# Both experts of a pair in one 16 KB home: 2 MB weight loads in a one-core decoder block

## The chip, the core and the metric

The kernel runs on one core of a Trainium2 chip. Its time is the device time of one execution in microseconds (us), the median of three runs. "MB" is 1,048,576 bytes and "KB" 1,024 where loads are counted; the profile's own GB/s and MB are decimal.

## What is computed

One decoder block on 256 tokens of width 1024, all in float32. Cut to what matters:

```python
h = rmsnorm(x, norm_mix_g) * (1 + scale_m) + shift_m           # scale, shift, gate from c @ w_ada
x = x + gate_m * mixer(h, positions, w_in, ...)                # mLSTM and retention, merged by gates
h = rmsnorm(x, norm_ffn_g) * (1 + scale_f) + shift_f
x = x + gate_f * moe(h, ...)
return rmsnorm(x, norm_final_g)

def moe(xm, ...):                                              # 32 experts, the best 4 for each token
    top_val, top_idx = lax.top_k(xt @ w_router + b_router, 4)
    top_w = softmax(top_val)
    # for each expert e, over the tokens that chose it
    gu = xb @ w_gate_up[e] + b_gate_up[e]                      # 1024 x 2048
    y = clamped_swiglu(gu) @ w_down[e] + b_down[e]             # 1024 x 1024
    # summed over each token's experts, weighted by top_w
```

The experts' weights are 32 x 12 MB = 384 MB and are read once.

## The kernel before, in words

The kernel has two stages. The first, up to line 1032, is the mixer with its modulation weights, the output projection and the routing. The second, from line 1035, runs over the 32 experts in 16 pairs. An expert has 64 slots for tokens; the pair's 128 slots fill PE's output rows, expert q in rows 64q to 64q+63.

**Homes.** All large weights go through one set of regions of 8 KB per partition, 1 MB each. There are 22 of them, named W0a, W0b, ... U6b, 11 names with two halves each. A table `ready` keeps a number for each half: the turn at which it was last filled or set free. `oldest` (line 138) returns the halves with the smallest numbers, whatever their names; `place` (line 129) puts a weight there, and `wslot` (line 144) places a weight of 2 MB in two halves and loads each with one DMA on SP's queue. The mixer's weights (w_in, the branches, wout, and the modulation weights wada) are loaded by `wslot`; in the mixer some halves also hold activations (U1 to U6, Z), and `free` enters them into the table when those are done. A load into a half waits until the last reader of what was there is done.

**The expert stage.** Each pair has four gate-and-up blocks (`gu`, n = 0 to 3) of 512 columns and two down blocks (`dn`, n = 0 and 1). A block is 4 MB: two experts, each with two halves of 1 MB (half h holds rows 512h to 512h+511 of the weight, as 128 partitions x 4 row groups x 512 columns). `both` (line 1156) takes four homes and issues four loads on SP, in the order (h=0,q=0), (h=0,q=1), (h=1,q=0), (h=1,q=1). In memory each of these is its own block of 128 rows of 8 KB. A name such as gu1531b in the profile is pair 15, block 3, expert 1, second half.

PE goes through k = 0 to 7 and, within each k, through q = 0, 1 (line 1204 for gate-and-up, 1245 for down): k = 0 to 3 read the first halves, k = 4 to 7 the second. Between the products PE turns the activations of the block before (`fill`), and in the second down block it gathers the next pair's tokens (`step`, line 1073). SP's order of loads in this stage and PE's order are as written in the code; the order of DVE and ACT in most of the mixer is not.

**The last pair.** Its first down block is loaded in eight pieces of 512 KB (runs of 4 KB, lines 1235 to 1239), its second one in sixteen pieces of 256 KB (runs of 2 KB) from a separate array `tail`, laid out so that its columns come in three cuts, `TAIL` (0 to 256, 256 to 384, 384 to 512). The output is normalised cut by cut (`finish`, line 1123).

**Overfull experts.** From line 1290 there is a branch for experts with more than 64 tokens. It repeats the work in a loop; in the profile it is skipped.

Of the kernel before, what the change touches and what calls it, by code (L numbers as in the profile page):

```python
# [10 lines left out]
F32 = mybir.dt.float32  # L11
# [9 lines left out]
D = 1024  # L21
T = 256
# [48 lines left out]
class Weight:  # L71


    def __init__(self, tiles, dim=1):
        self.tiles, self.dim = tiles, dim
# [11 lines left out]
class Pieces:  # L87


    def __init__(self, tiles, cuts):  # L90
        self.tiles, self.cuts = tiles, cuts

    def __getitem__(self, at):
        _, k, cs = at
        n, off = divmod(8 * cs.start, 2048)
        width = cs.stop - cs.start
        assert (cs.start, cs.stop) in self.cuts and off + 8 * width <= 2048
        off += k * width
        return self.tiles[n].rearrange("p a b -> p (a b)")[:, off:off + width]
# [3 lines left out]
def block(ctx, tc, I, out, dbg=None):  # L103
# [5 lines left out]
    big = ctx.enter_context(tc.tile_pool(name="big", bufs=1))  # L109
# [8 lines left out]

    ready = {f"W{i}{h}": 0 for i in range(4) for h in "ab"}
    clock = [0]  # L120

    def region(tag, shape, name, dt=F32, pool_=big):
        return pool_.tile(shape, dt, name=name, tag=tag)
# [5 lines left out]
    def place(tags, name, dim=1, pool_=big, cuts=((0, 512),)):  # L129
# [5 lines left out]
        tiles = [region(tag, half, name + h, pool_=pool_) for tag, h in zip(tags, "ab")]  # L135
        return Weight(tiles, dim) if len(cuts) == 1 else Pieces(tiles, cuts)
# [898 lines left out]
    w1, w2 = blocks_of("w1"), blocks_of("w2")  # L1035
# [120 lines left out]
    def both(src, name):  # L1156

        tags = oldest(4)
        w = [place(tags[q::2], f"{name}{q}") for q in range(2)]
        for h in range(2):  # L1160
            for q in range(2):
                ready[tags[2 * h + q]] = clock[0] + 0.25 * h
                sp.dma_start(flat(w[q].tiles[h]), src(q)(h))
        return w

    def gu(pair, n):
        return both(lambda q: w1(2 * pair + q, n), f"gu{pair}{n}")

    def dn(pair, n):
        return both(lambda q: w2(2 * pair + q, n), f"dn{pair}{n}")  # L1170
# [13 lines left out]
    for pair in range(NP):  # L1184
# [41 lines left out]
        for n in range(2):  # L1226
            if not last:
                w = dn(pair, n)
                cuts = ((0, 512),)
            else:  # L1230

                cuts = TAIL if n else ((0, 512),)
                w = [place(oldest(), f"dn{pair}{n}{q}", cuts=cuts) for q in range(2)]
                size = 512 if n else 1024
                for i in range(0, 4096, size):
                    for q in range(2):
                        h, c = divmod(i, 2048)
                        src = I["tail"][q, h] if n else w2(2 * pair + q, n)(h)
                        sp.dma_start(flat(w[q].tiles[h])[:, c:c + size], src[:, c:c + size])
            for c0, c1 in cuts:  # L1240
# [4 lines left out]
                for k in range(8):  # L1245
                    for q in range(2):
                        pe.matmul(p[q * CAP:(q + 1) * CAP, :c1 - c0], aT[:, k, q * CAP:(q + 1) * CAP], w[q][:, k, c0:c1],  # L1247
                                  start=False, stop=k == 7, skip_group_check=True)
# [28 lines left out]
        if pair == NP - 2:  # L1277
            tags = oldest()
            x2 = region(tags[0], [128, 2, D], "x2")
            gno = region(tags[1], [128, 2, D], "gno")  # L1280
            gn = gno[:, 0]
            for tag in tags:
                del ready[tag]
            waiting.append(lambda: row_of(cols[:, GFIN:GFIN + 8], gn, "gn", tr))
# [6 lines left out]
    with tc.If(more > 0):  # L1291
# [5 lines left out]
        with tc.For_i(0, E, 1) as e:  # L1297
# [3 lines left out]
            dve.tensor_copy(pcur, posm[:, :, ds(e, 1)].rearrange("p t o -> p (t o)"))  # L1301
            dve.tensor_copy(wcur, wm[:, :, ds(e, 1)].rearrange("p t o -> p (t o)"))
            dve.tensor_copy(sel, id3[:, ds(e, 1)].to_broadcast([96, CAP]))
            n_e = nc.values_load(nb[0:1, ds(e, 1)], min_val=0, max_val=T // CAP - 1)
            with tc.For_i(0, n_e, 1) as b:
# [21 lines left out]
                for n in range(4):  # L1327
                    w = wslot(lambda h: I["w1"][ds(e, 1), n, h].rearrange("o p c -> (o p) c"), f"gux{n}")
# [7 lines left out]
                    for q in range(2):  # L1336
                        pe.transpose(p[:, q * CAP:(q + 1) * CAP], a[:CAP, q * 128:(q + 1) * 128], ident[:CAP, :CAP])
                    act.activation(aT[:, 2 * n:2 * n + 2].rearrange("p k s -> p (k s)"), p[:, :2 * CAP], AF.Copy)
                for n in range(2):
                    ns = slice(n * 512, (n + 1) * 512)  # L1340
                    w = wslot(lambda h: I["w2"][ds(e, 1), n, h].rearrange("o p c -> (o p) c"), f"dnx{n}")
# [6 lines left out]
                    for t in range(2):  # L1348
                        pe.matmul(yacc[t][n], cwT[:, t * 128:(t + 1) * 128], yp, start=False, stop=True,
                                  skip_group_check=True)  # L1350

# [30 lines left out]
def arranged(inputs):  # L1382
# [17 lines left out]
    arrays["w1"] = halves(apart(I["w_gate_up"][0]))  # L1400
    w2 = I["w_down"][0]
    arrays["w2"] = halves(w2)
    last = w2[E - 2:, :, 512:].reshape(2, 8, 128, 512).swapaxes(1, 2)
    tail = [last[:, :, :, c0:c1].reshape(2, 128, -1) for c0, c1 in TAIL]
    tail = np.concatenate(tail, axis=2).reshape(2, 128, 2, 2048).swapaxes(1, 2)
# [20 lines left out]
```

## Time and profile before

| | us |
|---|---|
| three runs | 1266.93, 1266.97, 1268.28 |
| median | 1266.97 |
| the profiled execution | 1265.93 |
| its span, first to last instruction | 1263.8 |
| mean granted clock of TensorE | 0.993 of full speed |

The profile is of one execution. PE is TensorE's matmul, PEld its weight loads, DVE is VectorE, ACT ScalarE, SP the engine that issues the loads; "SPq" is its queue. A row of a timeline gives the start (us from the span's start), the duration, the engine and the line of the code, and the tile that is written, with what it reads. The duration of a DMA row is that of the issue on SP and not of the transfer. The chain of waits is followed back from the last instruction; a piece that is called DMA in it lasts from the issue of a load to its landing.

### The profile page before, as it was taken

What the parts mean: (1) busy time and instruction counts of PE and PEld (TensorE: products, weight loads), DVE (VectorE), ACT (ScalarE), POOL (GpSimd) and SP (SyncE); (2) the same over time, 40 slices, a digit from 0 to 9 for tenths busy, and PEclk for the clock granted to TensorE, in tenths of its full rate; (3) what the DMA queues carried; (4) which work ended last, traced back from release to release, by engine and by line L of the source; (5) the groups of instructions that cost most, each with busy time, mean ns of one, the idle gap of its engine ahead of it and who ended that gap; (6) DMA issues with size and microseconds to landing.
All of it is one profiled execution on the core that took longest, in us unless ns stands there. A gap on an engine that the chain in (4) does not pass through costs nothing.

```text
span 1263.8 us, 14948 instructions
## 1 busy us (share of the span) xinstructions
PE 1205.4 (95%) x5872; PEld 606.2 (48%) x5873; DVE 491.2 (39%) x1167; ACT 289.5 (23%) x559; POOL 3.9 (0%) x14
## 2 busy tenths in 40 slices
PE   8999999999899999999999999998999999999995
PEld 6878888878534334344343334343434333333333
DVE  5599889878422222222222222121212131222124
ACT  4585555565211101111010101010101011010111
POOL 0000000000000000000000000000000000000000
PEclk9999999999899999999999999999999999999998
DMA  9955788858799999999999999999999999999995
GB/s 363 362 185 212 291 291 330 360 203 332 274 422 422 421 420 422 421 420 420 421 422 421 422 421 421 421 422 421 421 421 421 421 421 421 422 421 420 421 410 183
DMA packets 72607, 479.13 MB, mean 379 GB/s; under 512 B 8786, under 2 KB 9746, under 8 KB 17492
## 3 DMA queue, kind: packets, MB, share of 16 engines
q1 hardware_dynamic: 71668, 477.54, 92.9%
q8 instruction: 47, 0.77, 0.2%
q10 hardware_dynamic: 864, 0.59, 0.2%
q14 instruction: 28, 0.23, 0.1%
HBM read 476.46 MB, written 1.05 MB: 378 GB/s over the span
## 4 chain that ended last, share of the span: by engine, by line
DMA 49%; PE 46%; DVE 3%; ACT 1%; issue 0%; SPq 0%; ACTq 0%; DVEq 0%
PE gup L1206 12%; PE dnp L1247 6%; PE xgp L1078 2%; DMA gu1331b<-in_w 2%; DMA gu511a<-in_w 2%; DMA gu911a<-in_w 2%; DMA dn511a<-in_w 2%; DMA dn911a<-in_w 2%; DMA gu1411b<-in_w 2%; DMA gu611a<-in_w 2%; DMA gu1011a<-in_w 2%; DMA dn811a<-in_w 2%; DMA dn1211a<-in_w 2%; DMA gu1231a<-in_w 2%; DMA gu1531b<-in_w 2%; DMA gu1131a<-in_w 2%
## 5 line engine op out<-in xcount | busy, mean ns | idle before, releaser
L1114 DVE TENSOR_SCALAR g<-gup 128x256 f32<-128x256 f32 x64 | 27.2, 425 | 354.6 <-PE gup L1206 354.6
L1195 ACT ACTIVATE aT<-aTp 128x256 f32<-128x256 f32 x64 | 24.6, 384 | 292.9 <-PE aTp L1194 292.9
L1078 PEld LDWEIGHTS xgp<-oh,x 128*128 128x128 f32 x512 | 63.5, 195 | 51.4 <-issue 26.0
L1115 ACT ACTIVATE sg<-g 128x256 f32<-128x256 f32 x64 | 26.7, 417 | 256.2 <-DVE g L1114 253.0
L1084 DVE TENSOR_SCALAR xg<-xgp,fsc,fsh 128x128 f32<-128x128 f32 x64 | 26.2, 409 | 149.1 <-ACT xg L1086 149.1
L1078 PE MATMUL xgp<-oh,x 128*128 128x128 f32 x512 | 75.5, 292 | 1.0 <-DVE oh L1070 1.0
L1254 DVE SCALAR_TENSOR_TENSOR yp<-dnp,wsl,gf 128x512 f32<-128x512 f32 (+2 forms) x34 | 24.5, 719 | 113.0 <-PE dnp L1247 110.9
L1086 ACT ACTIVATE xg<-xgp,fsh,fsc 128x128 f32<-128x128 f32 x64 | 29.0, 454 | 156.6 <-PE xgp L1078 156.6
L1264 ACT ACTIVATE yph<-yp 128x512 fp32r<-128x512 f32 x31 | 19.5, 629 | 94.7 <-DVE yp L1254 94.7
L1194 PEld LDWEIGHTS aTp<-ca,a 128*128 128x128 f32 x128 | 13.8, 141 | 39.5 <-issue 39.5
L1118 DVE TENSOR_TENSOR a<-a,sg 128x256 f32<-128x256 f32 x64 | 27.2, 425 | 8.2 <-ACT sg L1115 1.0
L1270 PE MATMUL ya<-yph,ohT 128*128 128x512 f32 x62 | 27.8, 449 | 1.5 <-ACT yph L1264 1.5
L1117 DVE SCALAR_TENSOR_TENSOR a<-a,g 128x256 f32<-128x256 f32 x64 | 27.2, 425 | 2.1
L1194 PE MATMUL aTp<-ca,a 128*128 128x128 f32 x128 | 27.4, 296 | 0.0
L1116 DVE TENSOR_SCALAR a<-gup 128x256 f32<-128x256 f32 x64 | 26.6, 415 | 0.0
L1265 DVE TENSOR_TENSOR ypl<-yp,yph 128x512 fp32r<-128x512 f32 x31 | 21.4, 689 | 11.9 <-ACT yph L1264 11.9
L1104 DVE TENSOR_SCALAR ohT<-cwp 128x256 fp32r<-128x256 f32 x16 | 6.8, 425 | 48.7 <-PE cwp L1103 48.7
L202 PE MATMUL gup<-bex,id 96*64 96x512 bf16 x128 | 25.1, 387 | 0.0
L1270 PEld LDWEIGHTS ya<-yph,ohT 128*128 128x128 f32 x62 | 11.6, 187 | 28.2 <-issue 24.3
L1270 PE MATMUL ya<-ypl,ohT 128*128 128x512 f32 x62 | 24.6, 397 | 0.2 <-DVE ypl L1265 0.2
L202 PEld LDWEIGHTS <-id 96*64 96x64 bf16 x196 | 12.3, 109 | 23.9 <-issue 20.5
L1070 DVE TENSOR_SCALAR oh<-ca,posm,rc 128x64 f32<-128x64 f32 x64 | 17.0, 309 | 6.3 <-PE xgp L1078 6.3
(1280 smaller groups left out, 3223.8 us busy)
## 6 DMA issues: line engine op xcount, KB each, us to landing
x<-in_x SPq DMA_DIRECT2D x2, 512.0 KB
wada2a<-in_ada SPq DMA_DIRECT2D x2, 512.0 KB, 7.6
wada0a<-in_ada SPq DMA_DIRECT2D x2, 512.0 KB, 8.9
wfirst0a<-in_win SPq DMA_DIRECT2D x2, 512.0 KB, 10.6
wfirst1a<-in_win SPq DMA_DIRECT2D x2, 512.0 KB, 10.1
wada2b<-in_ada SPq DMA_DIRECT2D x2, 512.0 KB
wfirst2a<-in_win SPq DMA_DIRECT2D x2, 512.0 KB, 10.2
wada0b<-in_ada SPq DMA_DIRECT2D x2, 512.0 KB, 10.2
```

The source lines that it names most:

```text
L202: pe.matmul(p[rows, :c1 - c0], id3[:, e:e + 1].to_broadcast([96, CAP]), bex[:, n, c0:c1], start=True, stop=False, skip_group_check=True)
L1078: pe.matmul(p[:, q * 128:(q + 1) * 128], x[:, t, k * 128:(k + 1) * 128], oh[:, t].rearrange("p q s -> p (q s)"), start=t == 0, stop=t == 1)
L1086: act.activation(xg[:, k], pq, AF.Identity, bias=fsh[:, k:k + 1], scale=fsc[:, k:k + 1])
L1114: dve.tensor_scalar(g[:r], v[:, 0], LIMIT, None, op0=OP.min)
L1115: act.activation(sg[:r], g[:r], AF.Sigmoid, scale=ALPHA)
L1116: dve.tensor_scalar(a[:r], v[:, 1], LIMIT, -LIMIT, op0=OP.min, op1=OP.max)
L1117: dve.scalar_tensor_tensor(a[:r], a[:r], 1.0, g[:r], op0=OP.add, op1=OP.mult)
L1118: dve.tensor_mul(a[:r], a[:r], sg[:r])
L1194: pe.transpose(p[:, q * 128:(q + 1) * 128], a[:, q * 128:(q + 1) * 128], ident)
L1206: pe.matmul(p[q * CAP:(q + 1) * CAP], xg[:, k, q * CAP:(q + 1) * CAP], w[q][:, k], start=False, stop=k == 7, skip_group_check=True)
L1247: pe.matmul(p[q * CAP:(q + 1) * CAP, :c1 - c0], aT[:, k, q * CAP:(q + 1) * CAP], w[q][:, k, c0:c1], start=False, stop=k == 7, skip_group_c ...
L1270: pe.matmul(yacc[t][n], ohT[:, t * 128:(t + 1) * 128], part, start=pair == i == 0, stop=i == 1 and pair >= NP - 2, skip_group_check=True)
```

## The change

A home is now a whole name: 11 homes of 16 KB per partition. In the mixer `oldest` returns the two halves of the name whose later half has the smallest number. After the routing the set of regions is closed, and a new one, `pairs`, is opened with 11 tiles of 16 KB; `home` takes them in a fixed rotation, first the one that came free first. The weights of a pair are rearranged in memory (outside the timed kernel): half h of both experts lies in one block of 128 rows of 16 KB, expert 0's 8 KB and then expert 1's. A block (`block_of`) is loaded by two DMAs of 2 MB instead of four of 1 MB. `Pairs` finds expert q's rows in the tile. The last pair's first down block is loaded like every other, in two loads of 2 MB; its second one in eight pieces of 512 KB with runs of 4 KB, each of which holds both experts' part. `x2` and `gno` take one home of 16 KB where they took two of 8 KB. The branch for overfull experts loads an expert's half as two pieces and goes through pairs, with the two experts of a pair written out one after the other.

The diff, cut to its core:

```diff
+class Pairs:
+    def __init__(self, tiles):
+        self.tiles = tiles
     def __getitem__(self, at):
-        _, k, cs = at
...
+        q, k, cs = at
+        off = q * 2048 + k % 4 * 512
+        return self.tiles[k // 4][:, off + cs.start:off + cs.stop]
+
+class Pieces(Pairs):
+    def __getitem__(self, at):
+        q, k, cs = at
         width = cs.stop - cs.start
...
+        tile, off = divmod(8 * cs.start, 2048)
+        step, row = divmod(k, 512 // width)
+        off = (off if tile else 0) * 2 + step * 1024 + q * 512 + row * width
+        return self.tiles[tile][:, off:off + width]
...
-    def oldest(n=2):
-        return sorted(ready, key=lambda t: (ready[t], t))[:n]
+    def whole():
+        return {n: max(ready[n + "a"], ready[n + "b"]) for n in NAMES if n + "a" in ready and n + "b" in ready}
+
+    def oldest():
+        free = whole()
+        name = min(free, key=lambda n: (free[n], n))
+        return [name + "a", name + "b"]
...
-    w1, w2 = blocks_of("w1"), blocks_of("w2")
+    bctx.close()
+    pairs = ctx.enter_context(tc.tile_pool(name="pairs", bufs=1, reuse_waits="tile"))
+    queue = sorted(NAMES, key=lambda n: (whole()[n], n))
+
+    def pair_tile(tag, name):
+        return pairs.tile([128, 4096 + MORE.get(tag, 0)], F32, name=name, tag=tag)[:, :4096]
+
+    for name in NAMES:
+        pair_tile(name, f"pair{name}")
+
+    def home(name):
+        tag = queue.pop(0)
+        queue.append(tag)
+        return pair_tile(tag, name)
...
-    def both(src, name):
-        tags = oldest(4)
-        w = [place(tags[q::2], f"{name}{q}") for q in range(2)]
+    def block_of(src, name):
+        tiles = [home(f"{name}{h}") for h in "ab"]
         for h in range(2):
-            for q in range(2):
-                ready[tags[2 * h + q]] = clock[0] + 0.25 * h
-                sp.dma_start(flat(w[q].tiles[h]), src(q)(h))
-        return w
+            sp.dma_start(tiles[h], src[h])
+        return Pairs(tiles)
...
-                    pe.matmul(p[q * CAP:(q + 1) * CAP], xg[:, k, q * CAP:(q + 1) * CAP], w[q][:, k],
+                    pe.matmul(p[q * CAP:(q + 1) * CAP], xg[:, k, q * CAP:(q + 1) * CAP], w[q, k, slice(0, 512)],
...
-            if not last:
-                w = dn(pair, n)
-                cuts = ((0, 512),)
+            cuts = ((0, 512),)
+            if last and n:
+                cuts = TAIL
+                w = Pieces([home(f"tail{h}") for h in "ab"])
+                for h in range(2):
+                    for c in range(0, 4096, 1024):
+                        sp.dma_start(w.tiles[h][:, c:c + 1024], I["tail"][h, :, c:c + 1024])
             else:
-                cuts = TAIL if n else ((0, 512),)
-                w = [place(oldest(), f"dn{pair}{n}{q}", cuts=cuts) for q in range(2)]
-                size = 512 if n else 1024
-                for i in range(0, 4096, size):
-                    for q in range(2):
-                        h, c = divmod(i, 2048)
-                        src = I["tail"][q, h] if n else w2(2 * pair + q, n)(h)
-                        sp.dma_start(flat(w[q].tiles[h])[:, c:c + size], src[:, c:c + size])
+                w = dn(pair, n)
...
+    paired = lambda w: np.ascontiguousarray(w.reshape(E // 2, 2, -1, 2, 128, 2048).transpose(0, 2, 3, 4, 1, 5)).reshape(
+        E // 2, -1, 2, 128, 4096)
```

## Rows read from the trace of the kernel before

**Rows 1.** The page: busy PE, rate by slice, packets, one queue.

```profile
PE 1205.4 (95%) x5872; PEld 606.2 (48%) x5873; DVE 491.2 (39%) x1167; ACT 289.5 (23%) x559; POOL 3.9 (0%) x14
...
GB/s 363 362 185 212 291 291 330 360 203 332 274 422 422 421 420 422 421 420 420 421 422 421 422 421 421 421 422 421 421 421 421 421 421 421 422 421 420 421 410 183
DMA packets 72607, 479.13 MB, mean 379 GB/s; under 512 B 8786, under 2 KB 9746, under 8 KB 17492
...
q8 instruction: 47, 0.77, 0.2%
```

**Rows 2.** Windows: us, busy of PE, PEld, DVE, ACT, POOL; clock, DMA share, GB/s.

```profile
330.00:340.00 10.00, 10.00 (x54) 5.55 (x55) 3.01 (x11) 1.83 (x4) 0.00 (x0) 0.91 0.57 223
...
341.00:601.00 260.00, 258.79 (x1256) 97.60 (x1254) 67.97 (x178) 33.38 (x73) 0.00 (x0) 1.00 1.01 420
601.00:1226.00 625.00, 594.26 (x2668) 229.14 (x2664) 139.98 (x352) 64.94 (x147) 0.00 (x0) 1.00 1.01 421
...
1224.70:1236.30 11.60, 10.32 (x48) 3.13 (x45) 1.61 (x4) 1.18 (x3) 0.00 (x0) 1.00 0.95 365
```

**Rows 3.** The chain: start us, us, what; pairs 3 and 4, the passing-over, the last.

```profile
494.02 4.29 PE gup L1206 x20
...
546.33 4.29 PE gup L1206 x20
...
581.06 20.57 DMA gu511a<-in_w
...
1206.94 19.85 DMA gu1531b<-in_w
```

**Rows 4.** Issues on SP, every eighth load of the expert stage: start us, us.

```profile
1167.18 0.33 SPq L1163 DMA_DIRECT2D dn1411b<-in_w  x1
...
1187.06 0.33 SPq L1163 DMA_DIRECT2D gu1511b<-in_w  x1
...
1206.94 0.33 SPq L1163 DMA_DIRECT2D gu1531b<-in_w  x1
```

**Rows 5.** Issues on SP: the 22nd load of the expert stage and the 23rd.

```profile
323.74 0.76 SPq L1163 DMA_DIRECT2D dn011a<-in_w  x1
337.08 0.33 SPq L1163 DMA_DIRECT2D dn010b<-in_w  x1
```

**Rows 6.** Waits of PE from 60 to 330 us, the longest: total, times, longest.

```profile
PE pos L1026 <- DVE mask L1024: 1.8, 1, 1.8
```

**Rows 7.** Issues on SP at the start: first and last of ten 512 KB loads.

```profile
23.04 0.33 SPq L244 DMA_DIRECT2D wfirst0b<-in_win  x1
...
34.56 0.33 SPq L244 DMA_DIRECT2D wfirst2b<-in_win  x1
```

**Rows 8.** Issues on SP at the end; eight issues lie from each to the next.

```profile
1226.81 0.33 SPq L1239 DMA_DIRECT2D dn1501b<-in_w  x1
...
1236.84 0.33 SPq L1239 DMA_DIRECT2D dn1511a<-in_tail  x1
...
1242.01 0.33 SPq L1239 DMA_DIRECT2D dn1511b<-in_tail  x1
```

**Rows 9.** The chain, PE in the last pair's down blocks: start us, us, what.

```profile
1231.22 3.44 PE dnp L1247 x16
...
1235.02 3.79 PE dnp L1247 x16
...
1250.75 1.78 PE dnp L1247 x32
```

**Rows 10.** The tile gm: ns min/median/max, first and last start us, forms.

```profile
L310 DVE SCALAR_TENSOR_TENSOR gm<-wada4a,csil,gm x4: 745/748/752, 165.9 to 169.3; 128x512 f32<-128x512 f32 x4
...
L197 PE MATMUL rs<-gm,ones x4: 590/592/592, 265.6 to 266.9; 128*128 128x512 f32 x4
```

**Rows 11.** The tile o1b, its last reader.

```profile
L352 DVE TENSOR_TENSOR partsb<-o1b,partsa x4: 684/687/694, 163.6 to 167.4; 128x512 fp32r<-128x512 f32 x4
```

**Rows 12.** Issue on SP of the first half of wada4.

```profile
158.12 0.33 SPq L148 DMA_DIRECT2D wada4a<-in_ada  x1
```

More of the change, by code (lines that the diff above doesn't have):

```diff
@@ L84, in __getitem__ @@
         return self.tiles[n][tuple(at)]
-class Pieces:
-    def __init__(self, tiles, cuts):
-        self.tiles, self.cuts = tiles, cuts
+class Pairs:
+    def __init__(self, tiles):
+        self.tiles = tiles
     def __getitem__(self, at):
-        _, k, cs = at
-        n, off = divmod(8 * cs.start, 2048)
-        width = cs.stop - cs.start
-        assert (cs.start, cs.stop) in self.cuts and off + 8 * width <= 2048
-        off += k * width
-        return self.tiles[n].rearrange("p a b -> p (a b)")[:, off:off + width]
+        q, k, cs = at
[4 more added lines that the diff above has]
+        q, k, cs = at
+        width = cs.stop - cs.start
+        assert (cs.start, cs.stop) in TAIL
+        tile, off = divmod(8 * cs.start, 2048)
+        step, row = divmod(k, 512 // width)
+        off = (off if tile else 0) * 2 + step * 1024 + q * 512 + row * width
+        return self.tiles[tile][:, off:off + width]
 @with_exitstack
@@ L115, in f32v, with region @@
         return ap.bitcast(F32)
+    NAMES = ("W0", "W1", "W2", "W3", "Z", "U3", "U5", "U6", "U1", "U2", "U4")
     ready = {f"W{i}{h}": 0 for i in range(4) for h in "ab"}
+    MORE = {"U1": 4, "U2": 8, "U4": 8}
+    for name in NAMES:
+        for h in "ba":
+            size = 2048 + (MORE.get(name, 0) if h == "a" else 0)
+            big.tile([128, size], F32, name=f"first{name}{h}", tag=name + h)
     clock = [0]
-    def region(tag, shape, name, dt=F32, pool_=big):
-        return pool_.tile(shape, dt, name=name, tag=tag)
+    def region(tag, shape, name, dt=F32):
+        return big.tile(shape, dt, name=name, tag=tag)
     def free(*tags):
@@ L127, in free, with place @@
             ready[tag] = clock[0] + 0.5
-    def place(tags, name, dim=1, pool_=big, cuts=((0, 512),)):
+    def place(tags, name, dim=1):
         clock[0] += 1
@@ L134, in place @@
         half = [128, 4, 512] if dim == 1 else [128, 8, 256]
-        tiles = [region(tag, half, name + h, pool_=pool_) for tag, h in zip(tags, "ab")]
-        return Weight(tiles, dim) if len(cuts) == 1 else Pieces(tiles, cuts)
-    def oldest(n=2):
-        return sorted(ready, key=lambda t: (ready[t], t))[:n]
+        return Weight([region(tag, half, name + h) for tag, h in zip(tags, "ab")], dim)
+    def whole():
[4 more added lines that the diff above has]
+        return [name + "a", name + "b"]
     def flat(t):
@@ L1277, in block @@
         if pair == NP - 2:
-            tags = oldest()
-            x2 = region(tags[0], [128, 2, D], "x2")
-            gno = region(tags[1], [128, 2, D], "gno")
+            x2, gno = home("end").rearrange("p (i t d) -> i p t d", i=2, t=2)
+            queue.pop()
             gn = gno[:, 0]
-            for tag in tags:
-                del ready[tag]
             waiting.append(lambda: row_of(cols[:, GFIN:GFIN + 8], gn, "gn", tr))
@@ L1296, in block, with beyond, load @@
                 pe.matmul(yacc[t][n], zero, gf[:, :512], start=True, stop=True)
-        with tc.For_i(0, E, 1) as e:
+        def beyond(pr, q):
+            of = lambda ap: ap.rearrange("p t (r q) -> p t r q", q=2)[:, :, ds(pr, 1), q].rearrange("p t o -> p (t o)")
+            one = lambda ap: ap.rearrange("p (r q) -> p r q", q=2)[:, ds(pr, 1), q]
+            def load(name, n):
+                w = home(f"{name}{n}{q}").rearrange("p (k c) -> p k c", k=8)
+                for h in range(2):
+                    src = I[{"gux": "w1", "dnx": "w2"}[name]][ds(pr, 1), n, h, :, q * 2048:(q + 1) * 2048]
+                    sp.dma_start(flat(w[:, 4 * h:4 * h + 4]), src.rearrange("o p c -> (o p) c"))
+                return w
             pcur = s.tile([128, 2], F32, name="pcur", tag="pcur", bufs=1)
@@ L1300, in block @@
             sel = s.tile([96, CAP], BF16, name="selx", tag="selx", bufs=1)
[L1301 to L1304, printed above, removed]
+            dve.tensor_copy(pcur, of(posm))
+            dve.tensor_copy(wcur, of(wm))
+            dve.tensor_copy(sel, one(id3).to_broadcast([96, CAP]))
+            n_e = nc.values_load(one(nb[:, :E]), min_val=0, max_val=T // CAP - 1)
             with tc.For_i(0, n_e, 1) as b:
@@ L1327, in block @@
                 for n in range(4):
-                    w = wslot(lambda h: I["w1"][ds(e, 1), n, h].rearrange("o p c -> (o p) c"), f"gux{n}")
+                    w = load("gux", n)
                     p = at(f"gupx{n}")
@@ L1335, in block @@
                     p = tr(f"aTpx{n}")
-                    for q in range(2):
-                        pe.transpose(p[:, q * CAP:(q + 1) * CAP], a[:CAP, q * 128:(q + 1) * 128], ident[:CAP, :CAP])
+                    for j in range(2):
+                        pe.transpose(p[:, j * CAP:(j + 1) * CAP], a[:CAP, j * 128:(j + 1) * 128], ident[:CAP, :CAP])
                     act.activation(aT[:, 2 * n:2 * n + 2].rearrange("p k s -> p (k s)"), p[:, :2 * CAP], AF.Copy)
@@ L1340, in block @@
                     ns = slice(n * 512, (n + 1) * 512)
-                    w = wslot(lambda h: I["w2"][ds(e, 1), n, h].rearrange("o p c -> (o p) c"), f"dnx{n}")
+                    w = load("dnx", n)
                     p = at(f"dnpx{n}")
@@ L1350, in block @@
                                   skip_group_check=True)
+        with tc.For_i(0, E // 2, 1) as pr:
+            for q in range(2):
+                beyond(pr, q)
         for c0, c1 in zip(FIN, FIN[1:] + (D,)):
@@ L1399, in arranged @@
     arrays["bgu"] = np.ascontiguousarray(apart(I["b_gate_up"][0]).reshape(E, 4, 512).swapaxes(0, 1).reshape(128, 512))
-    arrays["w1"] = halves(apart(I["w_gate_up"][0]))
+    paired = lambda w: np.ascontiguousarray(w.reshape(E // 2, 2, -1, 2, 128, 2048).transpose(0, 2, 3, 4, 1, 5)).reshape(
+        E // 2, -1, 2, 128, 4096)
+    arrays["w1"] = paired(halves(apart(I["w_gate_up"][0])))
     w2 = I["w_down"][0]
[L1402 to L1405, printed above, removed]
+    arrays["w2"] = paired(halves(w2))
+    last = w2[E - 2:, :, 512:].reshape(2, 8, 128, 512)
+    tail = []
+    for c0, c1 in TAIL:
+        rows = 512 // (c1 - c0)
+        piece = last[..., c0:c1].reshape(2, 8 // rows, rows, 128, c1 - c0)
+        tail.append(piece.transpose(3, 1, 0, 2, 4).reshape(128, -1))
+    tail = np.concatenate(tail, axis=1).reshape(128, 2, 4096).swapaxes(0, 1)
     arrays["tail"] = np.ascontiguousarray(tail)
```

12 lines of the change are left out of this document (7 added, 5 removed).

## The prediction

> **What bounds the kernel now.** I read the page first: from the twelfth of the forty slices to the next to last the transfer rate is flat at 420 GB/s and a little over [rows 1]. PE's 95% says less, because the two stages have different limits, so next come the windows by stage. From 341 to 1226 us the DMA share is 1.01 at 420 to 421 GB/s, with TensorE's granted clock at 1.00 [rows 2]: the expert stage moves 384 MB at one steady rate.
>
> Then the chain of waits. PE works through a pair of experts in 52.3 us (494.02 to 546.33) as long as the weights lie ready, and the chain runs over PE. At 581 us it passes to transfers, and near the end it is transfers alone [rows 3]. A load starts when the one eight before it has landed, and three such loads start 19.88 us apart [rows 4]: eight of 1 MB in 19.88 us is **2.485 us for 1 MB**, so a pair's 24 MB take 59.6 us against PE's 52.3. From there on time is bytes over rate, and PE has 7 us per pair to spare.
>
> When did this stream start? The first 22 loads fill the 22 homes up to 323.74 us; then the queue waits until PE lets the first home go, at 337.08 [rows 5], and the engines run dry meanwhile (share 0.57 from 330 to 340 [rows 2]). So the stream begins at PE's first release, and all that PE does before it (the mixer, the routing) comes on top. In the mixer PE's longest waits are for DVE, the longest 1.8 us, and none is for a load [rows 6].
>
> **The change, part by part.** *The loads.* Up to the last gate-and-up load there are 15 x 24 + 16 = 376 MB; 22 are in place at the first release, so 354 MB follow: 354 loads of 1 MB before, 177 of 2 MB after. The bytes are the same. What halves is the number of runs: 128 of 8 KB, 8 for each of 16 engines, against 128 of 16 KB. A run is one packet now: 72607 packets less 17492 under 8 KB leave 55115 of 8 KB [rows 1], and the 376 loads alone need 48128.
>
> What does a run cost beyond its bytes? No row has a 16 KB load; loads of shorter runs give a line. At the start the weights come as 512 KB loads, 128 runs of 4 KB: from 23.04 to 34.56 us nine follow each other, **1.280 us** each [rows 7]. From two of these to one of 1 MB the bytes stay and the time falls from 2.560 to 2.485, so a load costs 0.075 us besides 1.205 us for each 512 KB. A 2 MB load is then 0.075 + 4 x 1.205 = 4.895 us instead of 4.970, and **177 x 0.075 = 13.3 us** go.
>
> The other end comes from the last loads. Eight landings of 4 KB runs, read from the issues that they release, lie between 1226.81 and 1236.84: 1.254 us each. Eight of 2 KB runs (256 KB) lie between there and 1242.01: 0.646 us [rows 8]. From 4 to 8 KB that makes a fixed cost of 2 x 1.254 - 2.485 = 0.023 us (177 x 0.023 = 4.1 us saved), from 2 to 4 KB 2 x 0.646 - 1.254 = 0.038 us (6.7 us saved). I take 13.3, because the nine loads of the start stand in an even stream of their own kind, while the last ones change size under way and the DMA share falls to 0.95 there [rows 2]. The 4.1 goes into the range. Nothing below zero follows from these rows; what would give it is a rival.
>
> *Fewer issues.* 12 instead of 24 per pair on SP, 0.33 us each [rows 4]. SP waits for a landing between any two, so this is worth nothing. Eight loads under way are now 16 MB, and three homes (6 MB) are left to PE. Home N needs load N-11 consumed; that landed three loads (14.7 us) before the landing that lets N start, and PE takes 52.3/12 = 4.4 us for each of a pair's 12 half blocks, so the home is free in time. If PE were further behind, the queue would only get shorter than eight; it is empty only when PE is 22 MB behind, as before.
>
> *Landing in pieces of 2 MB.* PE's order takes step k of one expert, then of the other, so it already needed both experts' 1 MB for nearly all of a half block: zero while the stream runs. It is not zero at the **last pair**, whose first down block came in eight pieces of 512 KB and now comes in two of 2 MB. Before: gate-and-up landed at 1226.79 (19.85 us after its issue [rows 3]), PE's first down product began at 1231.22, the second half at 1235.02, the end came 3.79 us later, at 1238.81 [rows 9]. After: the halves land 4.90 and 9.79 us behind the last gate-and-up load, so the second half begins at +9.8 where it began at +8.2 (1235.02 - 1226.79): **1.6 us lost**. From there the chain to the output is PE's and DVE's and unchanged. The last 4 MB, now eight pieces of 4 KB runs, land by +9.8 + 8 x 1.28 = +20.0; PE, done with the first down block at +9.8 + 3.8 = +13.6, takes up the last quarter 11.9 us after that (1250.75 - 1238.81 [rows 9]), so their faster landing hides behind PE and gains nothing.
>
> *Homes in the mixer.* Whole names only: the first half of the modulation weight wada4 moves from a home freed by 158.12 us, when its load starts [rows 12], to the home of o1, whose second half is read until a split that begins at 167.4 [rows 11]. Wada4 is first used at 165.9 [rows 10]. Its first half would start when o1's first half is done, some microseconds after 158, so DVE could stand for up to about 4 us; but DVE's order there is not written by hand, and the row it makes (gm) is read by PE only at 265.6 [rows 10]. I take nothing and keep 0 to +4. Into the experts a 2 MB load starts at the later of the two releases; the last homes (Z) still fill at 323.74, land some 10 to 12 us later, and the first release at 337.08 is PE's. Zero. The branch for overfull experts is longer and not entered: zero.
>
> **Sum:** -13.3 + 1.6 = -11.7 us. The profiled execution took 1265.93 (span 1263.8 and 2.1 around it), which gives 1254.2; the median of the runs is 1.0 above it, so I forecast **1255.3 us**.
>
> **The rivals.**
> 1. *The fixed cost is small and the stream near its ceiling.* For it: 4 KB and 8 KB runs differ by 1% only in the last loads [rows 8]. Against it: the even stretch of the start [rows 7]. It gives -4.1 + 1.6, 1264.5, or with the 2 KB rows' 6.7 us 1261.9. The Trainium skill, page "DMA: Bandwidth & Descriptors", section "Why small descriptors are slow (HBM only)", puts about 3 cycles on each packet; with the 850 MHz of its section "Where 436 GB/s comes from" that is, as an estimate, 8 x 3.5 ns = 0.028 us a load, 5.0 us in all and 1263.6. By that rule, the start's 0.075 is too large and the last loads' 0.023 about right.
> 2. *Nothing is saved: a 16 KB run travels as two packets of 8 KB.* The rate stays and the lump is paid at the old rate (2 x 4.97 - 8.2 = 1.7 us): 1268.7, no measurable change. Against it: instruction fetch has 47 packets for 0.77 MB, 16 KB each [rows 1], so packets of that size do travel.
> 3. *Slower: the engines read 16 KB runs less well than 8 KB runs.* The place is every load after 337 us; it decides from a load of about 4.975 us on, since 177 x 0.005 and the 1.7 us make 2.5 us, 0.2%. If a long run were handled at the rate of the 4 KB loads of the start, 2 MB would take 4 x 1.280 = 5.12 us: +26.6 + 1.7, 1295. For it speaks only that no 16 KB load is in the rows; against it, that the time per byte falls with every doubling. The Trainium skill, the same page, section "Latency and other measured facts", has copies losing up to half their rate when the rows of a tile lie a large power of two apart, from 512 KB up, and advises contiguous tiles. By it, a contiguous 2 MB block with rows 16 KB apart is safe; no run here shows it.
> 4. *The mixer's tighter homes hold DVE up by 4 us*, with the loads as forecast: 1259.3, still faster.
>
> **How the numbers follow.** Forecast 62%, rival 1 15% (half of it faster, half the same), rival 2 10%, rival 3 8%, rival 4 5%. About 0.2% (2.5 us, 1264.4 to 1269.5) is what a measurement can tell from no change. Faster: 62 + 5 + 7 = 74%. Same: 8 + 10 = 18%. Slower: 8%. The range leaves out rivals 2 and 3 (18%). Its low end, 1252, is the forecast with 0.006 us more per load and 2 us from the mixer's order; its high end, 1267, is rival 1 with that order against it. The forecast's own range is 1252 to 1259.
>
> **What would show it.** Right: loads of 2 MB starting 8 x 4.895 = 39.2 us apart every eighth, GB/s near 428 where it was 421, packets down by some 26000 (24064 of them in the 376 loads), and a stream that still begins near 337. The second half of the last pair's first down block should begin near 9.8 us after the last gate-and-up landing. PE should still have idle time in each pair (58.7 against 52.3 us). Wrong: 2 MB loads at 4.97 us (rival 2), or between 4.90 and 4.95 (rival 1); more than 128 packets a load; a first release that has moved by more than 2 us; or waits of PE inside the mixer for a load.

## The result, and the profile after

| | before | after |
|---|---|---|
| median of four runs, us | 1267.14 | 1252.9 (1251.71 to 1255.89) |
| ratio, with its 95% interval | | 0.9889 (0.9871 to 0.9908) |
| the profiled execution, us | 1265.93 | 1252.83 |
| its span, us | 1263.8 | 1251.0 |

The changed kernel is 1.1% faster. The forecast was 1255.3 us; the median lies 2.4 us below it and inside the range of 1252 to 1267. The page's lines that answer to [rows 1]:

```profile
GB/s 362 366 184 212 292 275 359 353 185 333 318 425 428 427 428 426 429 426 428 427 428 427 427 427 429 428 426 427 428 429 427 427 427 427 430 427 427 427 422 117
DMA packets 43518, 479.12 MB, mean 383 GB/s; under 512 B 5554, under 2 KB 6514, under 8 KB 12212
```

The shape is the same, with a flat rate from the twelfth slice on, but it is flat at 427 to 428 where it was at 421. The packets fall by 29089. The forecast's "some 26000" are among them: 24064 in the 376 loads and 1792 in the last pair's down blocks. Nearly all of the rest, 3232 packets under 512 B (8786 before, 5554 after), was not forecast. They are 16 for each of the 202 DMAs that are gone (188 of the 376, 6 and 8 in the last pair's two down blocks): each load has one small packet on each of the 16 engines.

The windows of the expert stage, columns as in [rows 2]:

```profile
341.00:601.00 260.00, 258.82 (x1254) 97.78 (x1252) 66.55 (x175) 31.67 (x71) 0.00 (x0) 1.00 1.01 427
601.00:1213.00 612.00, 562.12 (x2668) 204.70 (x2666) 140.01 (x352) 65.31 (x148) 0.00 (x0) 1.00 1.01 427
```

The issues on SP (start us, duration us), answering to [rows 4, 5]:

```profile
319.11 0.42 SPq L1196 DMA_DIRECT2D dn01a<-in_w  x1
333.82 0.33 SPq L1196 DMA_DIRECT2D dn01b<-in_w  x1
...
1131.53 0.33 SPq L1196 DMA_DIRECT2D dn141b<-in_w  x1
...
1170.69 0.33 SPq L1196 DMA_DIRECT2D gu153b<-in_w  x1
```

Two things are to be read here. From dn141b to gu153b eight loads of 2 MB start in 39.16 us, 4.895 us each, the figure of the forecast to the last digit. And the first release, which the forecast left at 337, came at 333.82.

The chain of waits in the last pair (start us, us, what), answering to [rows 3, 9]:

```profile
1141.32 39.10 DMA gu150b<-in_w
...
1180.48 39.17 DMA dn150b<-in_w
...
1219.79 3.67 PE dnp L1277 x16
...
1226.88 5.17 PE dnp L1277 x32
...
1237.10 1.78 PE dnp L1277 x32
...
1243.31 0.71 ACT end L1183
```

The last gate-and-up load lands at about 1209.80 (39.1 us after its issue at 1170.69; PE takes it up at 1209.84), so the second half of the first down block begins 10.0 us after that landing, where it was 8.2. The spans divide into three stretches:

| us | before | after | difference | forecast |
|---|---|---|---|---|
| start to the first release | 337.08 | 333.82 | -3.3 | 0 |
| from there to the last gate-and-up landing | 889.7 | 876.0 | -13.7 | -13.3 |
| from there to the end | 37.0 | 41.2 | +4.2 | +1.6 |

The middle stretch is the forecast's to within the spread between executions: in five profiles with the loads of the kernel before it lasts 887.4 to 889.7 us, in five with those of the changed one 875.6 to 876.3, 12.5 us less in the mean. The first and the last hold 3.3 us of gain and 2.6 us of loss that it did not have, and these nearly cancel. The experiments ask three things: is the middle the length of the runs, and not the size of a load or the homes; where do the 3.3 us come from; and what makes the end longer.

### The profile page after: what moved, and what is told of

Same layout as the page of the kernel before. It is cut to its first block, busy times and chain, and to the rows that moved or that the text cites. A ratio compares the mean times of both kernels' runs of the same rounds, so it can differ in the third digit from the quotient of the medians.

```text
span 1251.0 us, 14561 instructions
## 1 busy us (share of the span) xinstructions
PE 1172.1 (94%) x5872; PEld 582.7 (47%) x5873; DVE 490.9 (39%) x1167; ACT 289.4 (23%) x559; POOL 3.9 (0%) x14
## 2 busy tenths in 40 slices
DMA packets 43518, 479.12 MB, mean 383 GB/s; under 512 B 5554, under 2 KB 6514, under 8 KB 12212
## 4 chain that ended last, share of the span: by engine, by line
DMA 54%; PE 42%; DVE 2%; ACT 1%; issue 0%; SPq 0%; ACTq 0%; DVEq 0%
PE gup L1239 10%; PE dnp L1277 5%; DMA gu142b<-in_w 3%; DMA gu102b<-in_w 3%; DMA gu62b<-in_w 3%; DMA gu90b<-in_w 3%; DMA gu130b<-in_w 3%; DMA dn150b<-in_w 3%; DMA gu110b<-in_w 3%; DMA dn90b<-in_w 3%; DMA gu150b<-in_w 3%; DMA dn130b<-in_w 3%; DMA gu82b<-in_w 3%; DMA gu70b<-in_w 3%; DMA dn50b<-in_w 3%; DMA gu122b<-in_w 3%
## 5 line engine op out<-in xcount | busy, mean ns | idle before, releaser
L1227 PEld LDWEIGHTS aTp<-ca,a 128*128 128x128 f32 x128 | 13.7, 142 | 39.4 <-issue 39.4
```

Of the source, the lines that this page charges most:

```text
L1227: pe.transpose(p[:, q * 128:(q + 1) * 128], a[:, q * 128:(q + 1) * 128], ident)
```

## The experiments

Every kernel here computes the whole block. The kernel before ran beside each on the same chip; its median was between 1264.3 and 1267.1 us from one chip to the next, so ratios are what to compare.

**Length of the runs or size of the loads: three versions.** The first keeps the changed kernel's homes and its loads of 2 MB, but each load is two blocks with runs of 8 KB:

```diff
-            sp.dma_start(tiles[h], src[h])
+            sp.dma_start(tiles[h].rearrange("p (q c) -> p q c", q=2), src[h].rearrange("q p c -> p q c"))
...
-    paired = lambda w: np.ascontiguousarray(w.reshape(E // 2, 2, -1, 2, 128, 2048).transpose(0, 2, 3, 4, 1, 5)).reshape(
-        E // 2, -1, 2, 128, 4096)
+    paired = lambda w: np.ascontiguousarray(w.reshape(E // 2, 2, -1, 2, 128, 2048).transpose(0, 2, 3, 1, 4, 5))
```

> The changed kernel with its 16 KB homes, its 2 MB loads and its order, but each load reads two blocks of 128 rows of 8 KB, so it has 256 runs of 8 KB instead of 128 of 16 KB. Theory (the fixed cost belongs to the run): a 2 MB load takes 2 x 2.485 = 4.970 us again, 177 loads cost 13.3 us more, the span goes from 1251.0 to about 1264, and the packets rise by some 24000. Rival (the fixed cost belongs to the load, with its completion): 4.895 us stays or nearly so, and the span stays at 1251.

The second keeps the homes and makes two loads of 1 MB, runs of 8 KB, for each (same arrays):

```diff
-            sp.dma_start(tiles[h], src[h])
+            for q in range(2):
+                sp.dma_start(tiles[h][:, q * 2048:(q + 1) * 2048], src[h, q])
```

> The changed kernel, but each home is filled by two loads of 1 MB with 128 runs of 8 KB, as the kernel before filled two homes. Theory (cost by run): 4.970 us for a home, the same as two runs in one load, span about 1264. Rival (cost by load): also 4.970, so this run alone doesn't tell them apart; against the run with two runs in one load it does: equal by the theory, 13 us slower than it by the rival.

Measured: 1265.36 us, ratio to the kernel before 0.9998 (0.9988 to 1.0007), and 1264.78 us, 0.9992 (0.9982 to 1.0001). The page of the first, and below it the page and two issues of the second:

```profile
DMA packets 67838, 479.12 MB, mean 379 GB/s; under 512 B 5554, under 2 KB 6514, under 8 KB 12212
```

```profile
DMA packets 70880, 479.15 MB, mean 379 GB/s; under 512 B 8594, under 2 KB 9554, under 8 KB 15252
...
1086.37 2.77 SPq L1197 DMA_DIRECT2D dn130a<-in_w  x2
...
1200.76 2.77 SPq L1197 DMA_DIRECT2D gu153b<-in_w  x2
```

Splitting the runs alone adds 24320 packets to the changed kernel's 43518 and takes the whole gain back. In both versions the stretch from the first release to the last gate-and-up landing takes about 889 us again, as before (889.7), although the homes are the new ones. From dn130a to gu153b the second version fills 23 homes in 114.39 us, 4.973 us for 2 MB. Splitting the loads as well adds 3042 packets more, nearly all under 512 B, and changes nothing. So the price is one of runs, not of loads, and homes of 16 KB alone, without the longer runs, gain nothing in the stream.

**The line at a shorter run.** Four loads of 512 KB with runs of 4 KB for each home, from the first pair to the last:

```diff
-            sp.dma_start(tiles[h], src[h])
+            for c in (0, 1024):
+                for q in range(2):
+                    sp.dma_start(tiles[h][:, q * 2048 + c:q * 2048 + c + 1024], src[h, q, :, c:c + 1024])
```

> The changed kernel, but each home is filled by four loads of 512 KB with 128 runs of 4 KB. Theory with the fixed cost of the start's loads (0.075 us for 8 runs of an engine): 4 x 1.280 = 5.120 us for a home, 177 x 0.225 = 39.8 us more than the changed kernel, span about 1291. Rival with the cost that the last loads of the kernel before gave (1.254 us for 512 KB): 5.016 us for a home, 21.4 us more, span about 1272.

Measured, one run: 1288.78 us. Issues on SP, one group of four for each home, and the landing of the last gate-and-up load from the chain:

```profile
333.24 1.95 SPq L1198 DMA_DIRECT2D dn01b<-in_w  x4
...
603.21 4.11 SPq L1198 DMA_DIRECT2D gu52a<-in_w  x4
...
654.38 4.12 SPq L1198 DMA_DIRECT2D gu61a<-in_w  x4
...
1239.04 10.19 DMA gu153b<-in_w
```

Ten homes in 51.17 us are 5.117 us for 2 MB, against 5.120 by the loads of the start [rows 7] and 5.016 by the last loads [rows 8]. The last loads' 1.254 us was not the price of a steady stream. The stretch from the first release (333.24) to the last gate-and-up landing (1249.23) takes 916.0 us, 40.0 more than in the changed kernel, where the theory has 39.8. The span, 1287.0 us, is 4 us below the theory's 1291 because the end from that landing on takes 37.8 us and not 41.2.

**A longer run still.** Pairs 1 to 14 load 4 MB at a time, runs of 32 KB, into five homes of 32 KB; the last pair's first down block comes in pieces of 512 KB again:

```diff
-    queue = sorted(NAMES, key=lambda n: (whole()[n], n))
+    queue = ["q1", "q2", "q3", "q4", "q5"]
...
+            t, tiles = quad(name)
+            sp.dma_start(t, src.rearrange("p h c -> p (h c)"))
```

> The changed kernel with one step more: pairs 1 to 14 load a whole block (both halves, both experts) as one load of 4 MB, 128 runs of 32 KB, into five homes of 32 KB; pair 0 and the last pair keep loads of 2 MB, and the last pair's first down block comes in eight pieces as in the run with the tail in pieces. Theory (a fixed cost by run, 0.075 us for the 8 runs that an engine carries of a load): 4 MB take 0.075 + 8 x 1.205 = 9.715 us instead of 9.790, 84 loads save 6.3 us; coarser homes give back about 3 us at the start, where the first 4 MB wait for two half blocks; with the tail's 3.3 us the span is about 1244.5 and the time about 1246.5. Rival (nothing below 16 KB's cost is left, or the engines take a 32 KB run as two): 9.79 us a load, span about 1251. Second rival (five homes are too few): the load's period is longer than 9.8 us because a load waits for PE.

Measured: 1250.87 us, 0.9878 (0.9861 to 0.9895). Windows of the steady stretch and of the start:

```profile
601.00:1190.00 589.00, 541.25 (x2562) 199.12 (x2562) 134.30 (x338) 62.90 (x142) 0.00 (x0) 0.99 1.00 431
...
340.00:350.00 10.00, 9.53 (x46) 3.30 (x44) 3.68 (x11) 2.28 (x5) 0.00 (x0) 1.00 0.72 283
```

The rate is 431 GB/s. From the first load of pair 6 (612.37) to that of pair 14 (1081.14) a pair takes 58.6 us in the mean; the same eight pairs take 59.1 us each in the changed kernel (603.91 to 1076.78) and 60.0 in the kernel before (629.70 to 1109.81). These means hold short pauses that the even stretches leave out (in the changed kernel one gap of 5.72 us among gaps of 4.89, for example). The line gives 6 x (0.075 + 8 x 1.205) = 58.3 instead of 12 x 4.895 = 58.7, so the saving, 0.5 us a pair, is the line's. But with five homes the loads wait for PE when the stream begins, and the DMA share drops to 0.72 there. The time misses the theory's 1246.5 by 4.4 us, of which the last block's first cut explains 1.2 (4.70 us where 3.48 was expected); the rest was not taken apart. The ratio cannot be told from that of the changed kernel.

**The 3.3 us ahead of the first release.** PE's products in the mixer are shorter after the change, those of 128x512 that take the normalised input `ha`, `hb` as the stationary operand. The last set, before and after (tile view: ns min/median/max, first and last start):

```profile
L364 PE MATMUL gr_p<-partsa,ha x32: 392/397/400, 243.1 to 264.9; 128*128 128x512 f32 x32
...
L364 PE MATMUL bml_p<-partsa,yma x32: 389/389/499, 197.8 to 219.9; 128*128 128x512 f32 x32
```

```profile
L386 PE MATMUL gr_p<-partsa,ha x32: 389/389/389, 240.2 to 261.2; 128*128 128x512 f32 x32
...
L386 PE MATMUL bml_p<-partsa,yma x32: 389/389/499, 195.5 to 217.7; 128*128 128x512 f32 x32
```

The 96 products of the set take 21.0 us instead of 21.8. The products of the same form with `yma` take 389 ns in both. What differs is where the regions lie. By the memory layout of the built programs, `ha` starts at byte 187872 of a partition before (480 in its block of 512 bytes) and at 130432 after (384); `yma` at 114048 in both (384). So I moved `ha` in the kernel before, by widening one earlier region. `hb` and all regions behind them move along; the moving operands (`partsa`, `partsb`) and `yma` stay where they are. The first version puts it at byte 187904 (0 of 512):

```diff
-        U1a = region("U1a", [128, 2052], "U1a")
+        U1a = region("U1a", [128, 2064], "U1a")
```

> The kernel before with one region of the mixer (U1a) made 48 bytes per partition longer, so that the regions behind it, the normalised input that all mixer products hold still (ha, hb), start on a multiple of 64 bytes as in the changed kernel, where they stood 32 bytes past one; nothing else differs. Theory (the mixer is 3.3 us shorter because of that address): mixer products with ha fall from 397 to 389 ns, the first home is let go at about 333.8 instead of 337.08, time about 1263.7. Rival (the mixer is shorter because its homes and with them its order changed): 397 ns stay, 337.1 and 1267 stay.

Measured: 1261.66 us, 0.9962 (0.9948 to 0.9976); products of 392 to 398 ns, the first release at 335.25. In the profile that is half of the effect and fits neither theory: the products change with the address, and a multiple of 64 bytes does not bring 389 ns. The times don't show a half: this version is 4.5 us faster than the kernel before beside it. The second version gives the place in 512 that `yma` and the changed kernel have, 384 (byte 188288), by `[128, 2160]`:

> The kernel before with the same region made longer by 416 bytes more, so that ha and hb start 384 bytes past a multiple of 512, as they do in the changed kernel, as yma does in both (389 ns in both), and as the split weights do. 480 bytes past it (the kernel before) gave 397 ns, 0 (a multiple of 64 all the same) gave 393. Theory (the place within 512 bytes sets the products' time): 389 ns, the first home let go at about 333.8, 3.3 us less than the kernel before, time about 1263 beside a kernel before at 1266.2. Rival (alignment to 64 bytes explains half and the order of the mixer the rest): 393 ns and about 335.3 again.

Measured: 1262.46 us, 0.9972 (0.996 to 0.9984), 3.5 us faster than the kernel before beside it, with products of 389 ns in nearly all of the sets. By their times the two versions can't be told apart (the intervals overlap); that byte 384 is better than byte 0 rests on the products' durations and on one profile's first release. And the reverse, the changed kernel with `ha` 32 bytes further (130464, 416 of 512):

```diff
-    MORE = {"U1": 4, "U2": 8, "U4": 8}
+    MORE = {"U3": 8, "U1": 4, "U2": 8, "U4": 8}
```

> The changed kernel with one region (U3a) 32 bytes per partition longer, so that ha, hb and what lies behind them start 32 bytes past a multiple of 64, as in the kernel before; order and homes are those of the changed kernel. Theory (address): products with ha take 397 ns again, the first home is let go at about 337, span about 1254. Rival (order): 389 ns, 333.8 and 1251 stay.

Measured, one run: 1256.74 us. The last set and the first release in the kernel before with `ha` at 384, then in the changed kernel with it at 416:

```profile
L364 PE MATMUL gr_p<-partsa,ha x32: 389/389/389, 240.2 to 261.3; 128*128 128x512 f32 x32
...
333.80 0.33 SPq L1163 DMA_DIRECT2D dn010b<-in_w  x1
```

```profile
L386 PE MATMUL gr_p<-partsa,ha x32: 395/396/396, 242.8 to 264.5; 128*128 128x512 f32 x32
...
336.74 0.33 SPq L1196 DMA_DIRECT2D dn01b<-in_w  x1
```

Moving the address moves the first release by 3.3 us one way and by 2.9 us the other, with the homes and the order of the mixer as they were. Repeated executions of one program move it too, by 0.6 us in three pairs of profiles and by 2.5 us in a fourth, so the products' durations are the firmer evidence. The gain ahead of the stream is an accident of the layout: the new homes shifted `ha` to a better place.

**The end.** The changed kernel with the last pair's first down block in eight pieces of 512 KB:

```diff
-            sp.dma_start(tiles[h], src[h])
+            for c in (0, 2048, 1024, 3072) if fine else (None,):
+                cs = slice(0, 4096) if c is None else slice(c, c + 1024)
+                sp.dma_start(tiles[h][:, cs], src[h][:, cs])
...
+        return block_of(I["w2"][pair, n], f"dn{pair}{n}", fine=pair == NP - 1)
```

> The changed kernel, but the last pair's first down block comes in eight pieces of 512 KB with 4 KB runs, in the order in which PE needs them. The tail from the landing of the last gate-and-up load to the end is 41.2 us in the changed kernel and 37.0 before. Theory (PE stands still between the 2 MB lumps, 1.6 us late at the second half, and its granted clock then falls to 0.67 while the first cut's products run, 5.17 us instead of 3.48): both come back, tail about 37 to 38 us, the first cut's products at about 3.5 us with the clock at 1.00, span 1251.0 - 3.3 = about 1247.5. Rival (the slow first cut has another cause, such as the new layout of the tail's pieces): only the 1.6 us come back, the first cut's products stay at 5.2 us, span about 1249.4.

Measured: 1249.96 us, 0.9868 (0.9852 to 0.9883). In its profile the second half begins 8.2 us after the last gate-and-up landing and the first cut takes 3.48 us, as the theory has it. But the profiled execution was its slowest, 1253.23 us, and started the stream late (335.92), so both kernels ran once more, side by side:

> The changed kernel as it is, on the same chip as the next run, so that the two can be set side by side. Ratio to the kernel before about 0.989; tail from the last gate-and-up landing to the end about 41 us, the first cut's products at about 5.2 us with a granted clock well below 1.00.

> The run with the last pair's first down block in eight pieces of 512 KB once more, beside the changed kernel on one chip. Theory (pieces bring back the 1.6 us and the clock's 1.7 us): about 3.3 us, 0.26%, less than the run beside it, ratio to the kernel before about 0.986; first cut's products 3.5 us at clock 1.00. Rival (the earlier run's tail was that of one execution): no difference beyond the intervals, products at 5 us in this profile too.

Measured: the changed kernel 1252.95 us, 0.9902 (0.9885 to 0.9918); with the pieces 1251.0 us, 0.9896 (0.9877 to 0.9915). Their chains, the changed kernel first:

```profile
1179.57 39.09 DMA dn150b<-in_w
...
1218.80 3.67 PE dnp L1277 x16
...
1226.00 5.04 PE dnp L1277 x32
...
1242.31 0.71 ACT end L1183
```

```profile
1169.77 39.18 DMA gu153b<-in_w
...
1217.19 3.95 PE dnp L1279 x16
...
1224.56 3.48 PE dnp L1279 x32
...
1239.30 0.71 ACT end L1183
```

The last gate-and-up load lands at about 1208.9 in both (in the changed kernel two loads, 9.79 us, before dn150b), so the second half begins 9.9 us behind it with the lumps and 8.2 us with the pieces: the forecast's 1.6 us are there, and the pieces take them back. The first cut's 32 products add another 1.6 us, 5.04 against 3.48. In the medians the pieces gain 1.9 us where the theory had 3.3, and the two intervals overlap; the gain is shown in the chain and only suggested by the times.

**The slow first cut.** Why 5.04 to 5.17 us? The window of the changed kernel in its first profile (columns as in [rows 2]):

```profile
1227.00:1232.10 5.10, 5.02 (x32) 2.67 (x28) 2.96 (x8) 0.20 (x1) 0.00 (x0) 0.67 0.12 49
```

TensorE's granted clock has a mean of 0.67 there: part of the stretch was run at 1.2 GHz, not 2.4. My first reading was that PE stands still before the second lump (1.03 us until dn150b lands) and so loses its clock. Against it spoke the two versions of the kernel before with moved addresses: they have the pieces, and their first cuts took 4.99 and 4.82 us; so did the version with runs of 32 KB, 4.70. The kernel before and its version with `ha` at byte 384 ran once more, unchanged, to see whether one program shows both:

> The kernel before once more, unchanged. In its first profile the 32 products of the last block's first cut took 3.48 us at a granted clock of 1.00; in the changed kernel they took 5.17 and 5.04 us at about 0.67 to 0.70. Theory: the two 2 MB loads of the last pair bring the fall about, so the kernel before, which has pieces of 512 KB there, shows 3.5 us again. Rival: whether the clock falls there differs from execution to execution of the same program (two versions of the kernel before with only addresses moved showed 4.99 and 4.82 us): then 3.5 and about 5 us are both possible here, and 5 us would show it outright.

> The kernel before with the normalised input of the mixer at byte 384 of 512, once more, unchanged. Its first profile had the first cut's 32 products at 4.82 us. Theory of the two 2 MB loads: it has none, so that 4.82 is left unexplained by it, and it says nothing for this run. Theory of the program (each build has a fall or has none): about 4.8 to 5 us again. Rival, execution by execution: 3.5 us is possible, and would show it outright. The mixer's products at 389 ns and the first release near 333.8 should come back in any case.

Measured, one run each: 1266.71 and 1262.36 us; in the second the products take 389 ns and the first release is at 333.18 again. The kernel before, chain and window, in its first profile and in the new one:

```profile
1242.22 3.48 PE dnp L1247 x32
...
1242.20:1245.70 3.50, 3.47 (x34) 1.96 (x28) 3.08 (x8) 0.20 (x1) 0.00 (x0) 1.00 1.04 390
```

```profile
1234.35 3.87 PE dnp L1247 x16
...
1241.87 4.87 PE dnp L1247 x28
...
1240.00:1245.00 5.00, 4.78 (x24) 2.60 (x25) 4.10 (x9) 1.16 (x2) 0.00 (x0) 0.66 1.02 376
```

The unchanged program before, whose first profile had this cut at 3.48 us and a clock of 1.00, now has 4.87 us and 0.66; the other had 4.32 where it had 4.82. So the fall comes and goes between executions of one program, and it needs no lumps: the first reading falls. What decides it is open. In every profile PE stands still for 1.5 us shortly before this cut, waiting for ACT. All four profiles of kernels whose last pair has loads of 2 MB there show the fall (4.77 to 5.17 us), and five of the ten with smaller loads do (4.32 to 4.99 us, the others 3.48). That lumps make it likelier is not excluded by so few.

**The rest of the end.** ACT's last instruction and the last two output issues, `out` from the last home, in the kernel before, then the issues in the changed kernel and in the changed kernel once more (start us, duration us):

```profile
1256.96 0.71 ACT gno L1146
...
1258.01 1.20 SPq L1151 DMA_DIRECT2D out<-gno  x2
```

```profile
1244.35 1.70 SPq L1188 DMA_DIRECT2D out<-end  x2
```

```profile
1243.35 3.04 SPq L1188 DMA_DIRECT2D out<-end  x2
```

From the end of ACT's last instruction to the end of the span it is 6.1 us before (6.0 in the second profile), 7.0 and 8.3 us after. The other profiles agree: 5.8 to 6.3 us in the five of the kernel before and its versions, 6.7 to 8.3 in the nine of the changed kernel and its versions. The issues themselves are held longer; why was not tried.

## Why the prediction was right, point by point

- **What bounds the kernel**: held. The stream starts with PE's first release in both, and the time from there is bytes over rate. PE was not the bound at the higher rate: it is busy for 92% of 601 to 1213 us.
- **The loads**: right, -13.7 us where -13.3 was forecast (-12.5 in the mean of five profiles of each kind), and 4.895 us a load as forecast. The choice between the two ends of the bound (0.075 and 0.023 us) was the step on which the forecast stood, and it fell to the row from an even stream of its own kind. For 2 MB the runs gave 5.117 us at 4 KB, 4.973 at 8 KB, 4.895 at 16 KB in even stretches; at 32 KB only the means over eight pairs compare, 4.88 us against 4.93 at 16 KB and 5.00 at 8 KB. Each engine moves 32, 16, 8 and 4 runs in these (128 runs of a load over 16 engines), so a run costs some 9 to 11 ns (0.144 us for 16, 0.078 for 8, 0.043 for 4). The working put this price on "a load"; it is a price of the 8 runs that each engine moves for it, and the same for two loads of 1 MB and one of 2 MB with equal runs.
- **Fewer issues, eight loads of 2 MB in flight, pieces of 2 MB in the stream**: zero each, as forecast. The even 4.895 us leave no room for more.
- **The last pair**: the step itself was right, +1.8 us where +1.6 was forecast (10.0 - 8.2). The rest of the +4.2 was missing: 1.7 us are the first cut at the lower clock (5.17 against 3.48), which the kernel before shows too in its second profile, and 0.9 us the output's issues; 0.1 us came back in the second half's products. So the step that took the chain from there to the output as unchanged missed 2.5 us.
- **Homes in the mixer**: the step that failed. I took 0, bounded from 0 to +4, and it was -3.3. A first release that moves by more than 2 us was one of the prediction's own signs of being wrong. The working followed which home a weight goes to and when that home is free, and that part held. Wada4's first half starts at 162.4 instead of 158.1 and is first used at 167.5 instead of 165.9 [rows 10, 12]:

```profile
L332 DVE SCALAR_TENSOR_TENSOR gm<-wada4a,csil,gm x4: 744/746/750, 167.5 to 193.6; 128x512 f32<-128x512 f32 x4
```

  DVE waited 0.2 us for it. What the working left out is that new homes also move the activations' addresses. The lower bound of 0 excluded a gain without a reason: the rows gave none for a gain, but none against it either.
- **Rival 1** (a small fixed cost) fell with the steady 4.895 and 5.117 us. The Trainium skill, page "DMA: Bandwidth & Descriptors", section "Why small descriptors are slow (HBM only)", has about 3 cycles on each packet, by my estimate 0.028 us a load; these runs show 0.078 between 8 and 16 KB. So there is a price for each packet, as the page has it, but it is nearly three times as high.
- **Rival 2** (two packets for a run of 16 KB) fell: the 376 loads lost half of their packets. Runs of 32 KB are one packet each too: that version's page counts 32286 packets, as 128 for each load of 4 MB give.
- **Rival 3** (long runs read less well) fell: 428 GB/s at 16 KB and 431 at 32 KB. The Trainium skill, the same page, section "Latency and other measured facts", has a loss for rows a large power of two apart; in contiguous blocks with rows 16 or 32 KB apart these runs show no such loss.
- **Rival 4** (DVE held up by 4 us) fell: 0.2 us.

The medians agree better than the steps, and that is luck: -3.3 us of addresses and +2.6 us at the end, neither of them forecast, nearly cancel. The span fell by 12.8 us where 11.7 was forecast; the other 1.3 us of the median's 2.4 come from how the runs lie about the profiled execution.

## What to carry to other kernels

Where a stream of weights is the bound, take the price of a run from two even stretches with different runs, and multiply it by the runs that one engine moves; runs twice as long halve it, whether or not the loads become larger. When a change moves homes in memory, look at the durations of products whose operands only moved, before crediting anything else with the gain. At the end of the stream keep the pieces small, because the last block is paid from its landing on (1.7 us in the chain here).

## What the hardware showed that I had not expected

- The same product of 128x512 takes 389 ns with its stationary operand at byte 384 of 512 and about 393, 396 and 397 ns at 0, 416 and 480; over the mixer this is 3.3 us between 480 and 384. Other regions moved along with it, and four places make no rule.
- Each load has one small packet on each of its 16 engines, and 190 loads more or fewer (the versions with two runs and with two loads) changed no time that can be seen.
- In the full stream a load of 256 runs of 8 KB held SP itself for 4.56 us, one of 128 runs for 0.33. At the start of the stream the same load of 256 runs held it for 0.37, so the long hold belongs to the full stream and not to the load alone. Nothing waited for SP here (a load takes 4.97 us), so it cost nothing. Two issues of the version with two runs of 8 KB:

```profile
333.44 0.37 SPq L1196 DMA_DIRECT2D dn01b<-in_w  x1
...
1099.99 4.56 SPq L1196 DMA_DIRECT2D gu140b<-in_w  x1
```

- The granted clock fell for the first cut in some executions of a program and not in others, 1.4 us of 3.5 in the kernel before.
